# A hybrid attention and retention layer: x kept once until it is modulated, eight heads opened over the first ten k-tiles, and the later adaLN rows as one VectorE stream

## The chip, the cores and the metric

The kernel runs on one core of one Trainium2 chip. The metric is the device time of one execution, in microseconds. The kernel before was timed in three runs: 2550.24 us in the median, 2542.49 to 2552.98. A profiled execution of it stands beside these runs, and all rows below come from that one.

## The reference, cut to what matters

The layer takes 256 latent tokens `x` and 256 context tokens `ctx`, each 4096 wide, in float32:

```
mod = silu(c) @ ada_w + ada_b                       # 4096 -> 3 x 4096: shift, scale, gate
mod_c = silu(c_ctx) @ ada_w[:, :2*D] + ada_b[:2*D]  # shift and scale of the context
h  = rms_norm(x, norm_w)   * (1 + scale) + shift
hc = rms_norm(ctx, norm_w) * (1 + scale_c) + shift_c
proj = h @ w_in                                     # 4096 -> 14336: q, k, v, g of groups A and B
pc   = hc @ (the k and v columns of w_in)
o_d  = differential attention of 8 heads A (latent queries, latent and context keys)
o_r  = retention of 8 heads B (two directions, started from the context's state)
y = concat(o_d * silu(dg), o_r * silu(rg)) @ w_out
return x + gate * y
```

Every element of `h` needs its column's shift and scale, which are sums over all 4096 rows of `ada_w`. The matrices are read once: `ada_w` is 201 MB, `w_in` 235 MB, `w_out` 67 MB.

## The kernel before, in words

**Products.** Inputs are float32 and the products are kept near that precision by splitting each operand into a high and a low part (float32r) and adding three products: hi x hi, hi x lo and lo x hi. `h` is held transposed: 32 k-tiles of 128 rows (columns of the model) by 512 tokens, 256 of them latent and 256 context, in high and low parts (`hh`, `hl`). A tile of `h` is the stationary operand, and the weights stream past it. `prep` (L378) loads two k-tiles of weights into a `raw` buffer (three of them), one DMA for each of the two column segments, makes the high part on ScalarE (L390) and the low part by a subtraction on VectorE (L391), one k-tile at a time. `mm_unit` (L395 on) runs the three products (L404 to L406). A unit is two k-tiles of one head's columns. The k and v columns (kv) need all four row tiles of 128 tokens, the q and gate columns (qg) only the two latent ones; a head of A has 512 columns in each, one of B 384. Queues hold the DMA issues: nearly all loads are issued by SP, in order; stores and small loads by ScalarE's queue.

**Start.** `x` and `ctx` are loaded row by row (`load_x`), squared on ScalarE or VectorE for the norm, transposed on TensorE (L136), and written as a high and a low part into `hh` and `hl` (L363, L364). `rbc` holds each token's 1/rms in every partition.

**First stage, chunks of adaLN.** `K1` is 20: for the first 20 k-tiles shift and scale come from TensorE (`Ada`, L264): `CHUNKS` are 1, 1 and then nine times 2 k-tiles; a chunk has four groups of 16 small matmuls, then eight (`pm`, L280) that bring the sums to the columns' partitions. `modulate` (L283 on) turns a k-tile of x into a k-tile of h: L294 adds high and low part back together, L298 multiplies by norm and scale, ScalarE adds the shift (L299), VectorE forms the low part (L300). In between, the first `NS` = 5 heads of A run their kv units on each chunk as it comes (`SUnit`, L555 to L557); their sums are added up in SBUF by VectorE (L563), and the last head's stays in PSUM.

**Second stage, first parts.** The other 11 heads run kv over k-tiles 0 to 19 (`FIRST`, tiles psA5p to psB7p), and their sums go out to DRAM (`p_dram`). Meanwhile VectorE makes the adaLN sums of the last 12 k-tiles (`ada2_task`: three chunks of four k-tiles, 32 steps each; a step loads 512 KB of `ada_w` and does two accumulations of 128x1024, L325 and L327). At the end of a chunk 32 small matmuls (L335) close it. `between1` sets how many of its steps follow each unit.

**Third stage.** `SCHED`: for each head the kv units of the last 12 k-tiles, added to the stored part (L491, L499), and all 32 k-tiles of qg. The attention of one head (`attA`, `attB`) runs as a task of small steps between the units of the next. The gate (`gate_task`, L918 to L948) goes as VectorE accumulations of 128x512 beside the kv units only. Each head's output is transposed and stored to DRAM (`store_o`).

**Output.** The outputs are loaded back and split (`load_o`, L1015 and L1016), and 128 units run `w_out` with them (tile psO); `out_after` multiplies by the gate and adds x.

**What sets the order.** The program is written in one order; a scheduler works through a model of the time and, on each engine, issues the earliest instruction in program order that is ready, so that work may move ahead of its place where its buffers allow. On the chip each engine then goes strictly in the order found. Pools set the buffers: `a4` (9 places, for head sums, accumulators and outputs), `raw` 3, `whi` and `wlo` 4 single k-tiles, `adaw` 6, PSUM 6 banks for units and 2 for the rest.

Of the kernel before, what the change touches and what calls it, by code (L numbers as in the profile page):

```python
# [38 lines left out]
K1 = 20  # L39
CHUNKS = [1, 1] + [2] * 9  # L40
CHUNKS2 = [4, 4, 4]
LEAD = 0.3
NS = 5
ADAB = 6
RAWB = 3

FIRST = [f"A{h}" for h in range(NS, 8)] + [f"B{h}" for h in range(8)]
SCHED = []
for _h in range(8):
    SCHED += [f"kv A{_h}", f"qg A{_h}"]  # L50
SCHED += ["kv B0", "attB", "qg B0"]
for _h in range(1, 7):
    SCHED += [f"kv B{_h}", f"qg B{_h}"]
SCHED += ["kv B7"]
# [27 lines left out]
def hybrid_kernel(es, tc, x, c, ctx, c_ctx, norm_w, ada_w, ada_b, w_in, q_norm_w, k_norm_w,  # L82
# [12 lines left out]
    a4 = es.enter_context(tc.tile_pool(name="a4", bufs=9, side="right"))  # L95
# [4 lines left out]
    o_dram = dram.tile([HA + HB, P, 2, L], F32, name="o_dram")  # L100
# [3 lines left out]
    for k in "AB":  # L104
        for h in range(8):
            for i in range(2):
                p_dram[f"{k}{h}", i] = dram.tile([P, 2, 512 if k == "A" else 384], F32, name=f"p_dram{k}{h}_{i}")
# [9 lines left out]
    nc.scalar.dma_start(tab, ctab[:, 0:C_J])  # L117
# [21 lines left out]
    hA_cm = tc.tile_pool(name="hA", bufs=1, side="right")  # L139
    hA = hA_cm.__enter__()  # L140
    hB_cm = tc.tile_pool(name="hB", bufs=1, side="right")
    hB = hB_cm.__enter__()
    G = 4
    hh, hl = [], []
    for g in range(KT // G):
        pool = hA if g < KT // G // 2 else hB
        hh.append(pool.tile([P, G, 512], F32R, name=f"hh{g}"))
        hl.append(pool.tile([P, G, 512], F32R, name=f"hl{g}"))

    def h_hi(kt, a, b):  # L150
        return hh[kt // G][:, kt % G, a:b]

    def h_lo(kt, a, b):
        return hl[kt // G][:, kt % G, a:b]

    def load_x(rt):
        src = x if rt < 2 else ctx
        r0 = (rt % 2) * P
        ts = []
        for i in range(4):  # L160
            xt = a4.tile([P, 1024], F32, name=f"x{rt}_{i}", tag="a4")
            nc.sync.dma_start(xt, src[r0:r0 + P, i * 1024:(i + 1) * 1024])
            ts.append(xt)
        return ts

    xts = load_x(0)
# [20 lines left out]
    if True:  # L187
        sp = Carve(wpool.tile([P, 512], F32, name="setup0", tag="wlo", bufs=4))
        cr = sp.tile([64, P], F32, name="cr")
        nc.sync.dma_start(cr[0:32], c[0].rearrange("(k p) -> k p", p=P))  # L190
        nc.sync.dma_start(cr[32:64], c_ctx.rearrange("(k p) -> k p", p=P))
# [23 lines left out]
    c0s2 = [K1 + sum(CHUNKS2[:j]) for j in range(len(CHUNKS2) + 1)]  # L215

# [67 lines left out]
    def modulate(k0, cn, pm):  # L284
# [5 lines left out]
        for k in range(cn):  # L290
            kt = k0 + k
            t = adap.tile([P, 512], F32, name=f"hm{kt}", tag="hm")
            hi, lo = h_hi(kt, 0, 512), h_lo(kt, 0, 512)
            nc.vector.tensor_tensor(t, hi.bitcast(F32), lo.bitcast(F32), op=ALU.add)  # L294
            for s in range(2):
                a, b = s * 256, (s + 1) * 256
                sc, sh = md[:, k, 2 + s:3 + s], md[:, k, s:s + 1]
                nc.vector.scalar_tensor_tensor(t[:, a:b], t[:, a:b], sc, rbc[:, a:b], op0=ALU.mult, op1=ALU.mult)  # L298
                nc.scalar.activation(hi[:, a:b], t[:, a:b], AF.Identity, bias=sh)  # L299
                nc.vector.scalar_tensor_tensor(lo[:, a:b], t[:, a:b], sh, hi[:, a:b].bitcast(F32),  # L300
                                               op0=ALU.add, op1=ALU.subtract)

    def ada2_task():

        work = [(j, k) for j in range(len(CHUNKS2)) for k in range(KT)]
        ahead = []

        def load():
            if len(ahead) < len(work):
                j, k = work[len(ahead)]  # L310
                ahead.append(ada_load(c0s2[j], CHUNKS2[j], k, f"ada2_{j}_{k}")[0])

        for _ in range(ADAB - 1):
            load()
# [783 lines left out]
```

## Time and profile before

| what | value |
|---|---|
| median of three runs | 2550.24 us |
| the profiled execution's own time | 2548.96 us |
| its span, first to last instruction | 2547.1 us |
| mean granted clock of TensorE | 0.993 |
| TensorE busy | 2496.5 us |
| VectorE busy | 1718.8 us |
| ScalarE busy | 1000.9 us |
| moved by DMA | 563.70 MB, 221 GB/s over the span |

A line in the table of groups names line, engine, operation, the tile written and the tiles read, shapes and count; then busy time, mean of one in ns, and the engine's idle time before it. A busy TensorE is not one at its peak, since the ends of matmuls are modelled; how fast it goes is read from the distance of the starts.

### The profile page before, as it was taken

To read this page: it belongs to the slowest core of one execution; us is meant where nothing else is said; L and a number is where in the kernel's file an instruction comes from. 1 tells how busy PE (TensorE), PEld (TensorE's weight loads), DVE (VectorE), ACT (ScalarE), POOL (GpSimd) and SP (SyncE) were. 2 spreads that over 40 slices of the span, in tenths; PEclk is the share of its full clock that TensorE was granted. 3 is DMA by queue.
4 is the path that set the end of the run, shared out by engine and by line. 5 is a ranking of instruction groups with operands and counts; after the bars stand their busy time and mean duration, and the time that the engine had idled before them with its cause. 6 is when DMAs were issued, how large, how long until landed. Compare 5 with 4: busy or idle time off the path is not lost.

```text
span 2547.1 us, 36352 instructions
## 1 busy us (share of the span) xinstructions
PE 2496.5 (98%) x12634; PEld 2125.9 (83%) x12634; DVE 1718.8 (67%) x3028; ACT 1000.9 (39%) x2011; POOL 46.3 (2%) x49
## 2 busy tenths in 40 slices
PE   7899999999999999999999999999999999999999
PEld 4566667888999997788888888899999999788887
DVE  5555556965979546777877887777777666655554
ACT  5222222222323233354445444544444445444443
POOL 0000000000000000000000000000000000000000
PEclk8999999999999999999999999999999999999999
DMA  9989887865777438766776677556666556666765
GB/s 317 300 277 299 279 284 260 292 213 162 246 239 234 143 110 273 235 217 198 240 228 213 203 243 230 178 184 196 199 206 204 165 157 193 195 220 208 225 211 175
DMA packets 495159, 563.70 MB, mean 221 GB/s; under 512 B 31664, under 2 KB 385264, under 8 KB 494976
## 3 DMA queue, kind: packets, MB, share of 16 engines
q1 hardware_dynamic: 478208, 526.54, 65.9%
q10 hardware_dynamic: 16768, 34.85, 4.0%
q8 instruction: 99, 1.62, 0.3%
q14 instruction: 84, 0.69, 0.1%
HBM read 538.17 MB, written 23.09 MB: 220 GB/s over the span
## 4 chain that ended last, share of the span: by engine, by line
PE 90%; DMA 6%; DVE 2%; SPq 1%; issue 1%; ACT 1%; DVEq 0%; POOL 0%; ACTq 0%; POOLq 0%
PE psA L405 8%; PE psA L406 8%; PE psA L404 8%; PE psB L405 6%; PE psB L406 6%; PE psB L404 6%; PE psO L404 5%; PE psO L405 5%; PE psO L406 5%; DMA ada<-in_ada_w_dram 3%; PE pa L264 3%; DMA graw<-in_ada_w_dram 1%; PE psA3s L555 1%; PE psA1s L555 1%; PE psP L556 1%; PE psP L555 1%
## 5 line engine op out<-in xcount | busy, mean ns | idle before, releaser
L390 ACT CAST whiB<-rawB 128x384 fp32r<-128x384 f32 x512 | 259.6, 512 | 471.0 <-PE psB L406 197.9
L390 ACT CAST whiA<-rawA 128x512 fp32r<-128x512 f32 x412 | 253.9, 620 | 425.0 <-PE psA L406 242.0
L391 DVE TENSOR_TENSOR wloB<-rawB,whiB 128x384 fp32r<-128x384 f32 x512 | 279.2, 553 | 173.3 <-ACT whiB L390 169.7
L391 DVE TENSOR_TENSOR wloA<-rawA,whiA 128x512 fp32r<-128x512 f32 x412 | 281.8, 687 | 152.3 <-ACT whiA L390 147.9
L405 PE MATMUL psA<-wloA,hh 128*128 128x512 f32 x896 | 357.6, 399 | 2.1 <-DVE wloA L391 2.1
L406 PE MATMUL psA<-whiA,hl 128*128 128x512 f32 x896 | 355.5, 397 | 0.0
L404 PE MATMUL psA<-whiA,hh 128*128 128x512 f32 x896 | 319.2, 398 | 0.0
L405 PE MATMUL psB<-wloB,hh 128*128 128x384 f32 x896 | 303.7, 339 | 2.2 <-DVE wloB L391 2.2
L406 PE MATMUL psB<-whiB,hl 128*128 128x384 f32 x896 | 302.4, 337 | 0.0
L391 DVE TENSOR_TENSOR wloO<-rawO,whiO 128x512 fp32r<-128x512 f32 x256 | 175.6, 691 | 157.2 <-ACT whiO L390 156.9
L404 PE MATMUL psB<-whiB,hh 128*128 128x384 f32 x896 | 263.9, 339 | 1.2 <-ACT whiB L390 1.2
L390 ACT CAST whiO<-rawO 128x512 fp32r<-128x512 f32 x256 | 158.0, 620 | 200.0 <-PE psO L406 164.0
L327 DVE SCALAR_TENSOR_TENSOR acc<-ada,cT,acc 128x1024 f32<-128x1024 f32 x186 | 233.8, 1277 | 0.0
L937 DVE SCALAR_TENSOR_TENSOR gacc<-graw,cT,gacc 128x512 f32<-128x512 f32 x248 | 184.7, 745 | 51.5 <-DMA graw<-in_ada_w_dram 49.7
L405 PEld LDWEIGHTS psA<-wloA,hh 128*128 128x128 f32 x896 | 168.7, 188 | 42.7 <-DVE wloA L391 4.1
L405 PE MATMUL psO<-wloO,ohh 128*128 128x512 f32 x512 | 203.9, 399 | 0.0
L406 PE MATMUL psO<-whiO,ohl 128*128 128x512 f32 x512 | 203.5, 398 | 0.0
L404 PEld LDWEIGHTS psA<-whiA,hh 128*128 128x128 f32 x896 | 168.5, 189 | 39.7
L406 PEld LDWEIGHTS psA<-whiA,hl 128*128 128x128 f32 x896 | 168.7, 188 | 39.0
L405 PEld LDWEIGHTS psB<-wloB,hh 128*128 128x128 f32 x896 | 169.0, 189 | 4.4 <-DVE wloB L391 3.7
L406 PEld LDWEIGHTS psB<-whiB,hl 128*128 128x128 f32 x896 | 168.9, 189 | 0.3
L404 PE MATMUL psO<-whiO,ohh 128*128 128x512 f32 x512 | 164.0, 399 | 3.9 <-ACT ohh L1015 3.9
(395 smaller groups left out, 4213.3 us busy)
## 6 DMA issues: line engine op xcount, KB each, us to landing
ada<-in_ada_w_dram SPq DMA_DIRECT2D x512, 256.0 KB, 4.8
rawA<-in_w_in_dram SPq DMA_DIRECT2D x412, 256.0 KB, 3.2
rawB<-in_w_in_dram SPq DMA_DIRECT2D x256, 256.0 KB, 3.2
graw<-in_ada_w_dram SPq DMA_DIRECT2D x128, 512.0 KB, 4.9
rawO<-in_w_out_dram SPq DMA_DIRECT2D x128, 512.0 KB, 4.4
rawB<-in_w_in_dram SPq DMA_DIRECT2D x256, 128.0 KB, 2.9
p_dramA<-kvqgA ACTq DMA_DIRECT2D x16, 512.0 KB, 5.1
kvqgA<-p_dramA SPq DMA_DIRECT2D x16, 512.0 KB, 7.6
```

What stands on the lines that cost most here:

```text
L264: m = nc.tensor.matmul(self.pa[32 * g:32 * (g + 1), :], cpad[:, 2 * kt:2 * kt + 32], tiles[k], start=(u0 == 0 and i < 4), stop=(u0 + nk == ...
L327: nc.vector.scalar_tensor_tensor(acc[v], w, cv, acc[v], op0=ALU.mult, op1=ALU.add)
L390: nc.scalar.copy(hi, raw[:, k])
L391: nc.vector.tensor_tensor(lo, raw[:, k], hi.bitcast(F32), op=ALU.subtract)
L404: nc.tensor.matmul(pt[:, :ncol], a, hi, start=f, stop=False)
L405: nc.tensor.matmul(pt[:, :ncol], a, lo, start=False, stop=False)
L406: nc.tensor.matmul(pt[:, :ncol], b, hi, start=False, stop=e)
L555: nc.tensor.matmul(pt, a, hi, start=f, stop=False)
L556: nc.tensor.matmul(pt, a, lo, start=False, stop=False)
L937: nc.vector.scalar_tensor_tensor(acc, raw[:, k], cT[:, 0, kt:kt + 1], acc, op0=ALU.mult, op1=ALU.add)
```

## The change

The diff changes these things together.

- x is loaded by columns (`load_x`, all sixteen loads at once), squared on ScalarE, transposed, and copied once by VectorE into float32 tiles `raws` (two k-tiles each); `modulate` reads these and writes a new tile of `h` (high and low part, one place of `a4`). The tile of x is then free. The tiles of h come free one by one too.
- The pool `a4` has 39 places for all of it.
- `K1` is 10, `CHUNKS` 1, 1 and four times 2; `NS` is 8, so all heads of A open in the first stage.
- `Ada2` makes the adaLN sums of the other 22 k-tiles on VectorE: chunks of 2, 4, 4, 4, 4, 4 k-tiles. `spend` hands it an amount of time after each unit, and it goes as many steps as that pays for, by the costs `T_STEP`.
- `first_parts` goes over the heads (B kv, A qg, B qg, then A kv again) and gives each the k-tiles that are ready by then (`avail`); its sum is stored. `kdone` keeps how far each has come. What is left of the stream after that runs on its own.
- `rests` does the remaining k-tiles of every head, with all stored sums loaded and added (L499 before), the qg sums too.
- `prep` splits both k-tiles of a unit with one conversion and one subtraction; `whi` and `wlo` have three pairs.
- The gate goes in steps of 128x1024, spread evenly over all units of the third stage.
- The outputs of the B heads stay in SBUF as split tiles, and the output projection takes them first, the reloaded ones of A after them.

The diff, cut:

```diff
-K1 = 20
-CHUNKS = [1, 1] + [2] * 9
-CHUNKS2 = [4, 4, 4]
+CHUNKS = [1, 1] + [2] * 4
+K1 = sum(CHUNKS)
+LATER = [2, 4, 4, 4, 4, 4]
+
+FILL = 0.9
+T_COL = 0.457e-3
+T_STEP = {2: 1.49, 4: 2.55}
 LEAD = 0.3
-NS = 5
+NS = 8
...
+SLOTS = 39
...
-    nc.scalar.dma_start(tab, ctab[:, 0:C_J])
+    nc.sync.dma_start(tab, ctab[:, 0:C_J])
...
+    def load_x(src, i):
+
+        xt = a4.tile([P, 2, 512], F32, name=f"x{i}", tag="a4")
+        nc.sync.dma_start(xt, src[:, i * 512:(i + 1) * 512].rearrange("(r p) n -> p r n", p=P))
+        return xt
+
+    NX = D // 512
+    xts = [load_x(x, i) for i in range(NX)] + [load_x(ctx, i) for i in range(NX)]
...
             t = adap.tile([P, 512], F32, name=f"hm{kt}", tag="hm")
-            hi, lo = h_hi(kt, 0, 512), h_lo(kt, 0, 512)
-            nc.vector.tensor_tensor(t, hi.bitcast(F32), lo.bitcast(F32), op=ALU.add)
...
+                nc.vector.scalar_tensor_tensor(t[:, a:b], raw[:, a:b], md[:, k, 2 + s:3 + s], rbc[:, a:b],
+                                               op0=ALU.mult, op1=ALU.mult)
+            hs[kt] = a4.tile([P, 2, 512], F32R, name=f"h{kt}", tag="a4")
...
+        def steps(self):
+            for _ in range(ADAB - 1):
+                self.load()
+            for i, (c0, cn, k0) in enumerate(self.work):
+                n = cn * P
+                if k0 == 0:
+                    acc = [a4.tile([P, 2 * n], F32, name=f"acc{c0}_{v}", tag="a4") for v in range(2)]
+                for k, w in enumerate(self.ahead[i]):
...
+                    yield T_STEP[cn]
+                self.load()
+                if i + 1 == len(self.work) or self.work[i + 1][0] != c0:
...
+                    modulate(c0, cn, pm)
+                    self.avail = c0 + cn
+                    yield cn * 2.0 + 1.0
+
+        def spend(self, us):
+
+            self.credit += us
+            while self.credit > 0 and not self.done:
+                try:
+                    self.credit -= next(self.it)
+                except StopIteration:
+                    self.done = True
...
-        out_ = []
-        for k in range(nk):
-            hi = wpool.tile([P, ncol], F32R, name=f"whi{name}_{k}", tag="whi", bufs=4)
-            lo = wpool.tile([P, ncol], F32R, name=f"wlo{name}_{k}", tag="wlo", bufs=4)
-            nc.scalar.copy(hi, raw[:, k])
-            nc.vector.tensor_tensor(lo, raw[:, k], hi.bitcast(F32), op=ALU.subtract)
-            out_.append((hi, lo))
-        return out_
+        hi = wpool.tile([P, nk, ncol], F32R, name="whi" + name, tag="whi", bufs=3)
+        lo = wpool.tile([P, nk, ncol], F32R, name="wlo" + name, tag="wlo", bufs=3)
+        nc.scalar.copy(hi, raw)
+        nc.vector.tensor_tensor(lo, raw, hi.bitcast(F32), op=ALU.subtract)
+        return [(hi[:, k], lo[:, k]) for k in range(nk)]
...
+        if ada.pos == len(ada_units):
+            ada2.spend(0.3)
...
+    kdone = {(nm, qg): K1 if nm[0] == "A" and not qg else 0 for nm in heads for qg in range(2)}
+
+    def first_parts():
+
+        items = [(f"B{h}", 0) for h in range(HB)] + [(f"A{h}", 1) for h in range(HA)] + [(f"B{h}", 1) for h in range(HB)]
+        for nm, qg in items + [(f"A{h}", 0) for h in range(HA)]:
+            hd = heads[nm]
+            a, b = kdone[nm, qg], ada2.avail
+            if a < b and not (a > 0 and ada2.done):
+                kdone[nm, qg] = b
+                nrt = 2 if qg else 4
+                spare = FILL * 2 * 3 * nrt * hd.ncol * T_COL - (0.2 + 2 * hd.ncol * 1.05e-3)
+                for u in head_units(hd, qg, pairs(a, b), part=True, rest=a > 0, tag=f"p{a}"):
+                    yield u, lambda spare=spare: ada2.spend(spare)
+
+    run_units(first_parts())
+    while not ada2.done:
+        ada2.spend(1.0)
...
+        else:
+            o_t[slot] = a4.tile([P, 2, 2, L], F32R, name=f"o{slot}", tag="a4")
+            split(o_t[slot][:, 0], o_t[slot][:, 1], pt)
...
+    GW = 1024
+    GATE_STEPS = D // GW * (KT + 1)
...
+        gate_due[0] += GATE_STEPS / gate_due[1]
+        while gate_due[0] >= 1:
+            gate_due[0] -= 1
+            next(gate, None)
...
+    def rests():
+        for nm in [f"A{h}" for h in range(HA)] + [f"B{h}" for h in range(HB)]:
+            hd = heads[nm]
+            us = []
+            for qg in range(2):
+                a = kdone[nm, qg]
+                if a < KT:
+                    us.append(head_units(hd, qg, pairs(a, KT), rest=a > 0))
+                else:
+                    load_part(hd, qg)
...
+    order = list(range(HA, HA + HB - 1)) + list(range(HA)) + [HA + HB - 1]
```

## Rows read from the trace of the kernel before

**Rows 1.** The page's first part: span, and busy time of each engine.
```profile
span 2547.1 us, 36352 instructions
PE 2496.5 (98%) x12634; PEld 2125.9 (83%) x12634; DVE 1718.8 (67%) x3028; ACT 1000.9 (39%) x2011; POOL 46.3 (2%) x49
```

**Rows 2.** Table by stage: stretch and length in us, busy, clock, DMA share, GB/s.
```profile
0.00:50.00 50.00, 33.24 (x239) 23.26 (x239) 31.39 (x73) 33.56 (x65) 2.42 (x8) 0.85 1.03 318
50.00:140.00 90.00, 78.83 (x407) 51.02 (x404) 47.01 (x84) 20.24 (x38) 0.00 (x0) 0.95 0.97 308
140.00:434.00 294.00, 286.47 (x1449) 197.01 (x1448) 168.53 (x298) 66.34 (x118) 0.00 (x0) 1.00 0.87 280
434.00:603.00 169.00, 169.00 (x723) 135.87 (x722) 116.72 (x128) 43.90 (x73) 0.00 (x0) 1.00 0.68 220
603.00:941.00 338.00, 338.00 (x1965) 336.44 (x1964) 258.49 (x353) 103.47 (x212) 0.00 (x0) 0.99 0.65 203
```

**Rows 3.** TensorE in order of time, one chunk: start, length, operation, idle before.
```profile
221.47 1.92 PE L264 MATMUL pa<-ada,cpad 128*32 128x512 f32 x16
...
229.52 2.04 PE L264 MATMUL pa<-ada,cpad 128*32 128x512 f32 x16 [1.72 <-DMA ada<-in_ada_w_dram]
...
253.49 0.95 PE L280 MATMUL pm<-tab,ms 128*128 128x2 f32 x8
...
260.56 1.92 PE L264 MATMUL pa<-ada,cpad 128*32 128x512 f32 x16
```

**Rows 4.** TensorE in order of time, first parts: first and last of 67.
```profile
934.82 0.34 PE L405 MATMUL psB7p<-wloB,hh 128*128 128x384 f32 x1
...
946.26 0.34 PE L405 MATMUL psB7p<-wloB,hh 128*128 128x384 f32 x1
```

**Rows 5.** Chain that ended last, 900 to 1000 us: closing matmuls of a chunk.
```profile
906.79 3.46 PE pm L335 x32
```

**Rows 6.** Groups by line, VectorE.
```profile
L391 DVE TENSOR_TENSOR wloA<-rawA,whiA 128x512 fp32r<-128x512 f32 x412 | 281.8, 687 | 152.3 <-ACT whiA L390 147.9 <-DMA rawA<-in_w_in_dram 3.5
L391 DVE TENSOR_TENSOR wloB<-rawB,whiB 128x384 fp32r<-128x384 f32 x512 | 279.2, 553 | 173.3 <-ACT whiB L390 169.7 <-DMA ada<-in_ada_w_dram 1.5
L327 DVE SCALAR_TENSOR_TENSOR acc<-ada,cT,acc 128x1024 f32<-128x1024 f32 x186 | 233.8, 1277 | 0.0
L937 DVE SCALAR_TENSOR_TENSOR gacc<-graw,cT,gacc 128x512 f32<-128x512 f32 x248 | 184.7, 745 | 51.5 <-DMA graw<-in_ada_w_dram 49.7
...
L563 DVE TENSOR_TENSOR kvqgA<-psA1s,kvqgA 128x512 f32<-128x512 f32 x40 | 27.6, 689 | 35.2 <-PE psA1s L557 35.2
```

**Rows 7.** Groups by line, ScalarE.
```profile
L390 ACT CAST whiB<-rawB 128x384 fp32r<-128x384 f32 x512 | 259.6, 512 | 471.0 <-PE psB L406 197.9 <-PE psB3p L406 32.8 <-PE psB0p L406 30.0
L390 ACT CAST whiA<-rawA 128x512 fp32r<-128x512 f32 x412 | 253.9, 620 | 425.0 <-PE psA L406 242.0 <-PE psA6p L406 38.9 <-PE psA5p L406 36.4
```

**Rows 8.** DMA issues, 447 to 545 us (276 GB/s): KB each, us to landing.
```profile
DMA packets 19137, 27.00 MB, mean 276 GB/s; under 512 B 1600, under 2 KB 11072, under 8 KB 19130
...
rawA<-in_w_in_dram SPq DMA_DIRECT2D x36, 256.0 KB, 5.1
```

**Rows 9.** DMA issues, 610 to 850 us (239 GB/s).
```profile
DMA packets 48371, 57.28 MB, mean 239 GB/s; under 512 B 3808, under 2 KB 31968, under 8 KB 48352
...
rawB<-in_w_in_dram SPq DMA_DIRECT2D x55, 256.0 KB, 3.7
```

**Rows 10.** Table by stage for the instructions of tile acc alone.
```profile
500.00:550.00 50.00, 0.00 (x0) 0.00 (x0) 34.89 (x28) 1.00 0.83 267
550.00:600.00 50.00, 0.00 (x0) 0.00 (x0) 0.00 (x0) 1.00 0.36 114
```

**Rows 11.** Waits of TensorE, 434 us to the end: us in total, times, longest.
```profile
PE psO L404 <- ACT ohh L1015: 3.9, 1, 3.9
```

**Rows 12.** TensorE in order of time, a longer wait.
```profile
77.94 2.90 PE L264 MATMUL pa<-ada,cpad 128*32 128x512 f32 x16 [2.48 <-DMA ada<-in_ada_w_dram]
```

**Rows 13.** SP's queue in order of time: the two loads of a B unit.
```profile
1785.27 0.94 SPq L383 DMA_DIRECT2D rawB<-in_w_in_dram  x2
```

More of the change, by code (lines that the diff above doesn't have):

```diff
@@ L375, in hybrid_kernel @@
+        for r in range(2):
+            rt = 2 * half + r
+            dg = adap.tile([P, P], F32, name=f"dg{rt}", tag="hm")
+            nc.vector.tensor_scalar(dg, ident, rs[:, r:r + 1], None, op0=ALU.mult)
+            nc.tensor.matmul(pr[:, rt * P:(rt + 1) * P], ones, dg, start=True, stop=True)
+        ada.load()
+    ada.load()
     nc.scalar.copy(rbc, pr)
@@ L437, in run, with run_units @@
                 self.after()
-    def run_units(units, between=None):
-        for i, u in enumerate(units):
-            u.prepare()
-            if i + 1 < len(units):
-                units[i + 1].prepare()
+    def run_units(units):
+        it = iter(units)
+        nxt = next(it, None)
+        if nxt is not None:
+            nxt[0].prepare()
+        while nxt is not None:
+            (u, post), nxt = nxt, next(it, None)
+            if nxt is not None:
+                nxt[0].prepare()
             u.run()
-            if between is not None:
-                between(i)
+            post()
     class Bank:
@@ L603, in hybrid_kernel @@
     store_part(sheads[-1])
-    ada2 = ada2_task()
-    next(ada2)
-    n_units = len(FIRST) * K1 // 2
-    n_steps = len(CHUNKS2) * (KT + 1)
-    done = [0, 0]
-    def between1(i):
-        done[0] += 1
-        while done[1] < n_steps and done[1] < done[0] / (n_units - 10) * n_steps:
-            next(ada2, None)
-            done[1] += 1
-    for nm in FIRST:
-        run_units(head_units(heads[nm], 0, pairs(0, K1), part=True), between1)
-    for _ in ada2:
-        pass
+    kdone = {(nm, qg): K1 if nm[0] == "A" and not qg else 0 for nm in heads for qg in range(2)}
[13 more added lines that the diff above has]
+        ada2.spend(1.0)
     ada_cm.__exit__(None, None, None)
@@ L925, in gate_task @@
         for v in range(n):
[L926 to L937 removed]
+            cb, kt = divmod(v, KT)
@@ L967, in hybrid_kernel, with between @@
     gate = gate_task()
-    def gate_step():
-        next(gate, None)
-    def between(i):
+    atB = [None]
+    gate_due = [0.0, sum(len(pairs(a, KT)) for a in kdone.values()) - 8]
+    def between():
         bg_step()
@@ L1034, in hybrid_kernel, with load_o, out_ends, start @@
+    run_units(rests())
+    while next(gate, 0) is None:
+        pass
+    def load_o(slot):
+        stg = a4.tile([P, 2, L], F32, name=f"ostg{slot}", tag="a4")
+        nc.sync.dma_start(stg, o_dram[slot])
+        o_t[slot] = a4.tile([P, 2, 2, L], F32R, name=f"o{slot}", tag="a4")
+        split(o_t[slot][:, 0], o_t[slot][:, 1], stg)
     NB = D // 512
     final_units = []
-    def out_after(nb, bank):
-        def f():
+    def out_ends(nb, bank):
+        t = []
+        def start():
             gt = a4.tile([P, 512], F32, name=f"gt{nb}", tag="a4")
```

354 lines of the change are left out of this document (142 added, 212 removed).

## The prediction

> **What bounds it now.** I read the page's first part, then the table by stage, then the order of TensorE's instructions. The first shows TensorE busy for 2496.5 of 2547.1 us [rows 1]; the second shows where the other 51 us lie: 17 before 50 us, 11 from 50 to 140, 7.5 from 140 to 434, none from 434 to 941 [rows 2], so some 15 in all the rest. So two things can pay: less TensorE work, and the waits of the first 434 us. In that stretch DMA is at 0.87 of its engines or more (280 to 318 GB/s); afterwards, up to 941, at 0.65 to 0.68. VectorE is at 69% and 76% from 434 to 941 [rows 2].
>
> The prices. A 512-column matmul takes 0.234 us (720 weight matmuls, 30 units of 24, in 169 us) [rows 2]; a 384-column one 0.1733 (66 starts in 11.44 us) [rows 4]. A unit (two k-tiles) is then 5.62 us for kv and 2.81 for qg of an A head, 4.16 and 2.08 of a B head. A chunk of two k-tiles lasts 39.1 us (221.47 to 260.56): 120 weight matmuls, 28.1; four adaLN groups of 16 at about 1.95, 7.8; eight pm matmuls, 0.8; that leaves 2.4 us, 1.7 of it a wait for an adaLN load [rows 3].
>
> **The change, part by part.**
>
> *adaLN leaves TensorE.* Five of nine two-tile chunks go: 5 x (7.8 + 0.8) = **-43 us**. The VectorE stream gets ten more k-tiles, whose closing matmuls (32 in 3.46 us [rows 5], eight per tile) cost 80 x 0.108 = **+9**. The weight and output matmuls keep their number; when they run is what changes.
>
> *The chunk stage* reads the same 8.4 MB of ada_w per chunk, but beside eight heads instead of five: 12.6 MB in 192 x 0.234 + 8.6 = 53.5 us, 235 GB/s, where 11.0 MB in 39.1 us were 282. The waits of 140 to 434 should go; the earlier ones, where one-tile chunks follow the start, partly stay. Bounds 0 and -18.5 (both idle times of [rows 2]); I take **-10**.
>
> *The start.* Until 50 us DMA is at 1.03 of its engines [rows 2], and the same x, first chunk and weights must arrive before the first weight matmul. That x goes through one VectorE copy and shorter squares takes work off ScalarE and VectorE, which have 33.6 and 31.4 us there; DMA covers it. All x loads now stand before the first adaLN load on SP's queue, which delays the one as much as it advances the other; the loads of c pass to ScalarE's queue and the table to the head of SP's, ahead of x, some 0.1 MB. **0**, bounds -3 and +3. L294's adds leave VectorE, beside TensorE: 0.
>
> *Weight split by pairs.* One conversion and one subtraction replace two each. From the two widths [rows 6, 7] the slopes are 0.84 ns an element on ScalarE and 1.05 on VectorE, so a pair costs 1.05 and 1.22 us (A), 0.83 and 0.96 (B), against 1.37 and 1.11 on VectorE before. Off the path: 0 by itself, but it sets the loop below.
>
> *First parts.* By the kernel's own accounting (spare time per unit: 3.78 us A kv, 2.78 B kv, 1.25 A qg, 0.89 B qg) I followed which k-tiles are ready when each head starts: 44 units B kv, 60 A qg, 72 B qg, 52 second parts of A kv; 794 us of TensorE. What is new is 132 qg units in a row beside the adaLN stream. A raw buffer comes back only after its subtraction, and there are three: issue of two loads (0.94 [rows 13]), landing, conversion, subtraction, and that over three is the fastest unit. Landing is 3.7 us at 239 GB/s [rows 9] and 5.1 at 276 [rows 8]. B qg wants 0.39 MB per 2.08 us (189 GB/s), some 100 of the stream and 20 of stores: more than either row. With 3.7 us its loop is (0.94 + 3.7 + 0.83 + 0.96)/3 = 2.14 us, with 5.1 it is 2.61; over 72 units +4 and +38, and if each subtraction also stands behind one accumulation of 1.28 us [rows 6], 3.04 us and +69. Nothing in the trace has such a run of short units with a stream. The load is nearest to the 276 GB/s row, but the list of the stream is elastic (a late unit leaves it more room), so I take **+20**, bounds 0 and +69. A qg: (0.94 + 5.1 + 1.05 + 1.22)/3 = 2.77 against 2.81: **+2**, bounds 0 and +15. The second parts of A kv take four adds of 0.69 us [rows 6] before their banks come free, with only two spare banks: **+3**, bounds 0 and 8. What is queued behind a late adaLN tile on VectorE is the next weight subtraction, and TensorE waits for that.
>
> *The end of the stream.* Its cost is 64 x 0.745 + 160 x 2.55 + 50 for the modulations = 506 us; the budgets hand out 44 x 2.78 + 60 x 1.25 + 72 x 0.89 + 52 x 3.78 + 3 = 461. Some 43 us of VectorE work stand behind the last first part, with the next head's subtractions behind them. But the stream doesn't keep to its place in the program: before, 33 steps that are meant to last until past 603 were finished at 550 [rows 10]. VectorE's whole work there is 112 x 1.22 + 116 x 0.96 = 248 of subtractions, 22 of adds and 506 of stream, 776 against 794 + 20 on TensorE, and in the last chunks it has idle time too. So I take **+3** for the last modulation, bounds 0 and +42.
>
> *The rest.* Sixteen qg sums are stored, loaded and added; A kv once more. 32 additions on VectorE, which has fewer subtractions to do; loads on SP and stores on ScalarE's queue come four units early: 0. The gate is spread over the qg units also: a B qg unit with 0.54 steps of 0.52 MB is at some 290 GB/s, as above, but six or eight such units stand between kv units twice as long, and three split pairs are ahead: 0, bound +14. The a4 pool has 39 places: after the first parts 10 k-tiles of h are dead, so 22 + two heads (6) + gate (4) fit, and at the end 20 + 6 + 4 + seven finished outputs: 0. In the output projection the wait of 3.9 us for the reloaded last head [rows 11] goes, since B's outputs stay on the chip: **-4**, bounds -4 and +2. POOL's powers are two instead of four, and nothing new waits for them: 0.
>
> **Sum.** -43 + 9 - 10 + 20 + 2 + 3 + 3 - 4 = -20. The profiled execution took 2548.96 us, 1.9 more than its span; so 2529 by it, and 1.3 more by the median of the runs (2550.24): **2530 us**.
>
> **The rivals.**
> A. *All hidden*: the loop keeps up, because a raw tile that is asked for early lands as in the 239 GB/s row. -43 + 9 - 18 - 4 = -56 at best, with small losses -35: 2494 to 2515. For it: no idle from 434 to 941 with VectorE at 76% [rows 2]. Against: those units are twice as long. 0.2.
> B. *The stream ends late*: VectorE can't run ahead, because adaLN buffers or DMA hold it. Then up to 42 stand bare, while the B qg loop, with less beside it, costs 10: -20 - 10 + 39 = +9, 2559; half of it, 2540. 0.13.
> C. *Slower*: the loop of B qg decides alone. From 2.08 + 0.75 = 2.83 us per unit on (each subtraction behind an accumulation at 5.1 us landing gives 3.04) it costs 54 to 69 instead of 20: 2564 to 2579. The place is the stretch with 72 B qg units. 0.14.
> D. *The clock*: waits in that stretch could be long enough to slow TensorE. After a wait of 2.48 us the next adaLN group took 2.90 us [rows 12], after one of 1.72 us 2.04 [rows 3], so short waits cost nothing here, long ones do; a loop 0.3 to 0.9 us late per unit stays under both. If all 72 units ran at half the clock, 72 x 2.08 = 150 more: 2680. 0.03. The Trainium skill (TensorE: Matmul & The Clock Gate, HAM oscillation) tells of a matmul with little work per load whose every load wait put the engine back to half its clock, so that each step began cold; that speaks against thin units beside a stream. By it the sum would be D's, by the rows it is mine.
> E. *The first stage gains nothing*: DMA still limits it, because the first one-tile chunks need as many bytes and their waits grow. -10 falls away and some 5 are added: 2545. 0.05.
>
> **From cases to numbers.** The forecast's own range is 2515 to 2545, 0.45. About 0.5% (12.8 us) is what a measurement of this kernel can tell from no change: faster ends at 2537.5, slower begins at 2563. Faster: 0.2 (A) + 0.34 of the forecast + 0.01 of B = 0.55. Same: 0.11 of the forecast + 0.11 of B + 0.05 (E) = 0.27. Slower: C, D and 0.01 of B = 0.18. The range leaves out about a tenth on either side: 2495 to 2572.
>
> **What would show it.** Right: adaLN groups on TensorE 24 instead of 44; the chunk stage over at about 325 us with under 2 us idle per chunk; acc instructions well ahead of their heads; B qg first units at some 2.35 us each with raw loads landing in 4 to 5 us; no wait over 10 us at the last pm. Wrong: B qg at 2.8 us or more (C); TensorE idle for tens of us while VectorE accumulates, after the last A kv part (B); granted clock under 0.95 between 600 and 850 us (D); idle over 15 us before 320 us (E); first parts without idle (A).

## The result, and the profile after

The changed kernel takes 2660.06 us (median of 4 runs, 2654.71 to 2661.88) where the kernel before took 2550.88 (4 runs on the same chip, 2542.49 to 2552.98): 1.043 times as long, 95% interval 1.040 to 1.046. I had forecast 2530 and a range up to 2572. The profiled run took 2661.34 us, 112 more than that of before, at a span of 2659.6.

The page of the changed kernel, its first part, beside [rows 1]:

```profile
span 2659.6 us, 33974 instructions
PE 2515.6 (95%) x12354; PEld 2140.1 (80%) x12354; DVE 1820.5 (68%) x2438; ACT 887.6 (33%) x1384; POOL 42.7 (2%) x47
```

TensorE has 280 matmul records fewer, and is still busy 19 us longer: part of that time was spent at the lower clock (mean granted clock 0.969, before 0.993). It is idle for 144 us where it was idle for 51. The table by stage of the changed kernel (columns as in [rows 2]) says where:

```profile
0.00:50.00 50.00, 33.55 (x225) 21.74 (x226) 27.38 (x62) 26.13 (x74) 1.61 (x6) 0.83 1.05 320
50.00:140.00 90.00, 86.90 (x449) 58.02 (x448) 55.99 (x91) 24.95 (x41) 0.00 (x0) 0.98 0.94 295
140.00:250.00 110.00, 110.00 (x543) 76.74 (x542) 63.39 (x92) 22.11 (x27) 0.00 (x0) 1.00 0.78 249
250.00:350.00 100.00, 98.35 (x452) 81.94 (x451) 91.13 (x136) 23.01 (x30) 0.00 (x0) 1.00 0.78 263
350.00:1160.00 810.00, 794.84 (x3877) 693.74 (x3877) 630.16 (x639) 255.36 (x321) 2.90 (x1) 1.00 0.78 256
...
1186.00:1220.00 34.00, 24.98 (x91) 19.70 (x91) 28.53 (x50) 7.72 (x12) 0.00 (x0) 0.75 0.33 103
1220.00:1282.00 62.00, 41.88 (x140) 30.14 (x139) 47.36 (x63) 15.04 (x35) 2.50 (x1) 0.78 1.03 366
1842.00:1945.00 103.00, 47.88 (x191) 36.33 (x192) 60.28 (x133) 31.26 (x81) 5.82 (x7) 0.65 0.22 81
```

The first five rows are what the prediction was about, and they went much as forecast. The last three are three stalls, all in or at the third stage, for which the forecast had 3 us. What a stretch loses I read as its length less busy time times granted clock (an estimate, since the ends of matmuls are modelled): 34 - 24.98 x 0.75 = 15 us, 62 - 41.88 x 0.78 = 29 and 103 - 47.88 x 0.65 = 72. Together 116 us.

**Stall 1, 1186 to 1220: the stream's end.** TensorE in order of time (start, length, operation, idle before):

```profile
1197.06 0.79 PE L406 MATMUL psA<-wloA,h 128*128 128x512 f32 x1 [4.08 <-DVE wloA L393]
...
1204.49 6.56 PE L330 MATMUL pm<-ones,acc 128*128 128x1 f32 x30 [0.84 <-DVE acc L322]
```

The third stage has begun, its units wait for weight subtractions that stand behind the last accumulations on VectorE, and the last closing matmuls run at the lower clock (0.50 from 1204 to 1212): 30 take 6.56 us where 32 took 3.46 [rows 5].

**Stall 2, 1220 to 1282: a burst on the queue.** DMA issues of the changed kernel from 1233 to 1282 us (KB each, median us to landing):

```profile
DMA packets 8001, 19.09 MB, mean 390 GB/s; under 512 B 696, under 2 KB 4223, under 8 KB 7997
...
graw<-in_ada_w_dram SPq DMA_DIRECT2D x21, 512.0 KB, 9.1
rawA<-in_w_in_dram SPq DMA_DIRECT2D x16, 256.0 KB, 8.3
kvqgA<-p_dramA SPq DMA_DIRECT2D x8, 512.0 KB, 9.2
```

The gate's loads, meant as one every other unit, come 21 in 49 us, and with them 8 stored sums for several heads at once. A weight load takes 8.3 us to land where it took 5.1 at 276 GB/s [rows 8]. TensorE waits up to 6.4 us for a conversion (the first of the waits below; 14.2 of its 17.6 us lie here).

**Stall 3, 1842 to 1945: A7's attention, alone.** The attentions run one after another, as a chain in which each is a link; one stands bare when no unit's matmuls run beside it. Each attention of an A head has one long power on POOL near its start, so POOL's instructions in order of time are a list of them (start, length; the last row is near the end of A7's):

```profile
1265.12 2.50 POOL L749 TENSOR_TENSOR rsA<-rsA,mhalf 128x12 f32<-128x12 f32 x1 [120.38 <-DMA graw<-in_ada_w_dram]
...
1648.23 2.58 POOL L749 TENSOR_TENSOR rsA<-rsA,mhalf 128x12 f32<-128x12 f32 x1 [9.76 <-DVE rsA L748]
...
1859.78 2.58 POOL L749 TENSOR_TENSOR rsA<-rsA,mhalf 128x12 f32<-128x12 f32 x1 [7.14 <-DVE rsA L748]
...
1896.77 0.54 POOL L826 TENSOR_TENSOR stA<-stA,mhalf 128x1 f32<-128x1 f32 x1 [2.17 <-DVE stA L825]
```

The same rows of the kernel before, first and last of eight:

```profile
1039.66 2.56 POOL L736 TENSOR_TENSOR rsA<-rsA,mhalf 128x12 f32<-128x12 f32 x1 [92.73 <-DVE rsA L735]
...
1657.12 2.58 POOL L736 TENSOR_TENSOR rsA<-rsA,mhalf 128x12 f32<-128x12 f32 x1 [9.79 <-DVE rsA L735]
```

And TensorE's instructions on the third stage's sums, changed kernel (times, first and last start):

```profile
L405 PE MATMUL psA<-whiA,h x560: 387/397/796, 1163.5 to 1646.2; 128*128 128x512 f32 x187
...
L405 PE MATMUL psB<-whiB,h x896: 332/336/689, 1646.9 to 2278.9; 128*128 128x384 f32 x180
```

Before, A's sums ran from 956 to 1648 us (692), and the eight attentions started one every 88 us: when the sums ended, the last attention was just starting (1657). After, A's sums last 484 us, but the attentions still start one every 85 us ((1859.78 - 1265.12) / 7); beside A's sums it is even 96 ((1648.23 - 1265.12) / 4), and 71 after them. When A's sums end at 1647, the fifth of the eight attentions is just starting. TensorE runs ahead with B's sums for 195 us and then stops, until A7's attention is over and B's have begun, which the program puts behind it. The waits of the changed kernel (us in total, times, longest; the first three of TensorE in the whole span, the last of SP's queue from 1842 to 1960):

```profile
PE psA L405 <- ACT whiA L392: 17.6, 7, 6.4
PE kTpA L132 <- DVE kvqgA L718: 12.2, 1, 12.2
PE psA L406 <- DVE wloA L393: 11.9, 8, 4.1
...
SPq L387 <- DVE nlbB L862: 59.0, 1, 59.0
```

The second is TensorE at the start of A7's attention. The last is SP's queue from 1842 on: the next weight load stands for 59 us, as VectorE makes no weight subtraction between 1843 and 1901, only A7's steps. From 1842 to 1930 TensorE runs no unit.

### The profile page after: what moved, and what is told of

The parts are those of the page before. It is cut to its first block, busy times and chain, and to the rows that moved or that the text cites. A ratio compares the mean times of both kernels' runs of the same rounds, so it can differ in the third digit from the quotient of the medians.

```text
span 2659.6 us, 33974 instructions
## 1 busy us (share of the span) xinstructions
PE 2515.6 (95%) x12354; PEld 2140.1 (80%) x12354; DVE 1820.5 (68%) x2438; ACT 887.6 (33%) x1384; POOL 42.7 (2%) x47
## 5 line engine op out<-in xcount | busy, mean ns | idle before, releaser
L322 DVE SCALAR_TENSOR_TENSOR acc<-ada,cT,acc 128x1024 f32<-128x1024 f32 (+1 forms) x372 | 427.9, 1190 | 0.0
L406 PE MATMUL psB<-wloB,h 128*128 128x384 f32 x896 | 305.2, 341 | 2.4 <-DVE wloB L393 2.4
L407 PE MATMUL psB<-whiB,h 128*128 128x384 f32 x896 | 303.3, 339 | 0.0
L405 PE MATMUL psB<-whiB,h 128*128 128x384 f32 x896 | 285.1, 340 | 5.7 <-DVE kvqgB L500 5.7
L406 PE MATMUL psA<-wloA,h 128*128 128x512 f32 x560 | 229.4, 410 | 12.0 <-DVE wloA L393 11.9
L405 PE MATMUL psA<-whiA,h 128*128 128x512 f32 x560 | 212.8, 405 | 17.6 <-ACT whiA L392 17.6
L407 PE MATMUL psA<-whiA,h 128*128 128x512 f32 x560 | 226.0, 406 | 0.0
L406 PE MATMUL psO<-wloO,o 128*128 128x512 f32 x512 | 204.1, 399 | 0.3 <-DVE wloO L393 0.3
L407 PE MATMUL psO<-whiO,o 128*128 128x512 f32 x512 | 203.4, 398 | 0.0
L405 PE MATMUL psO<-whiO,o 128*128 128x512 f32 x512 | 184.3, 399 | 1.2 <-ACT o L722 1.2
L952 DVE SCALAR_TENSOR_TENSOR gacc<-graw,cT,gacc 128x1024 f32<-128x1024 f32 x124 | 158.8, 1281 | 38.7 <-DMA graw<-in_ada_w_dram 37.6
L405 PEld LDWEIGHTS psB<-whiB,h 128*128 128x128 f32 x896 | 167.7, 190 | 7.5 <-DVE kvqgB L500 6.1
L406 PEld LDWEIGHTS psB<-wloB,h 128*128 128x128 f32 x896 | 169.3, 189 | 4.9 <-DVE wloB L393 4.0
L407 PEld LDWEIGHTS psB<-whiB,h 128*128 128x128 f32 x896 | 169.4, 189 | 0.5
```

The costliest lines, as they stand in the source:

```text
L322: nc.vector.scalar_tensor_tensor(acc[v], w, cv, acc[v], op0=ALU.mult, op1=ALU.add)
L405: nc.tensor.matmul(pt[:, :ncol], a, hi, start=f, stop=False)
L406: nc.tensor.matmul(pt[:, :ncol], a, lo, start=False, stop=False)
L407: nc.tensor.matmul(pt[:, :ncol], b, hi, start=False, stop=e)
L952: nc.vector.scalar_tensor_tensor(acc, raw, cT[:, 0, kt:kt + 1], acc, op0=ALU.mult, op1=ALU.add)
```

## The experiments

Sixteen kernels; each time stands beside runs of the kernel before on the same chip (2550 to 2553). "Changed" is 2660, and "less" and "more" are against it where nothing else is named. Kernels 5 and 6 leave out part of the layer's work, and so return another result.

**1. The pace of the attention steps.**

```diff
-        bg_step()
-        if len(tasks) > 1:
+        for _ in range(3):
             bg_step()
```

> Three attention steps are issued behind every unit instead of one or two. Theory P (the pace of issue sets the length of the chain of attentions): A's eight attentions, some 79 us each in the changed kernel (1265 to 1900), shrink to about 60, the length of a head's sums, A7's attention no longer runs alone after 1842, and the time falls by 55 to 75 us, to about 2595. Theory C (the chain is long because its dependent instructions stand in line behind other work on VectorE, ScalarE and TensorE, and A's sums of the third stage, 484 us instead of 690, are too few to cover it): 70 to 76 us each, A7 still alone for about 40 us, and the time falls by 10 us at most: 2650 to 2660.

2705.24 us: 45 more, outside both. The first and the last power of A's attentions on POOL, and the table by stage of this run:

```profile
1265.72 2.50 POOL L749 TENSOR_TENSOR rsA<-rsA,mhalf 128x12 f32<-128x12 f32 x1 [118.89 <-DMA kvqgA<-p_dramA]
...
1829.96 2.58 POOL L749 TENSOR_TENSOR rsA<-rsA,mhalf 128x12 f32<-128x12 f32 x1 [7.13 <-DVE rsA L748]
```

```profile
1800.00:1920.00 120.00, 59.98 (x238) 45.95 (x239) 69.15 (x150) 35.05 (x90) 5.82 (x7) 0.64 0.21 76
1960.00:2400.00 440.00, 407.34 (x2205) 383.99 (x2204) 268.92 (x397) 141.79 (x213) 6.50 (x12) 0.93 0.58 188
```

A7 is still alone, and earlier. The attentions start 81 us apart instead of 85, so theory P is out: issuing them sooner hardly shortens them. What neither theory had is the second row: B's part loses 440 - 407.34 x 0.93 = 61 us. In the changed kernel the same stretch loses 22 (426.88 us busy at 0.98). It goes in dents of 5 to 10 us, most at a change of B heads; in this stretch TensorE waits 9.6 us for conversions, 5.9 for subtractions and 9.1 for the rope of B's attentions on VectorE (L881). I read it as the run ahead with B's sums being shorter here (145 us instead of 195); that wasn't tested alone.

**2. The gate late.**

```diff
-        gate_due[0] += GATE_STEPS / gate_due[1]
+        if atB[0] is not None:
+            gate_due[0] += GATE_STEPS / gate_due[1]
```

(and the divisor counts B's units alone)

> The gate's steps are issued only after the change to B's attentions, one per unit, none beside A's units. Theory G (the gate's burst of 32 loads and accumulations makes the stall of 1233 to 1282): that stretch loses its 20 us of idle time and its half clock, and the time falls by 25 to 40 us, to about 2630. It also takes 1.28 us accumulations out of VectorE's line, so the attentions of A should take about 72 us each instead of 79. Rival (the stall comes from the switch to 24-matmul units with their stored sums to add, not from the gate): no change there, 2650 to 2665. In B's part VectorE takes 164 us more beside some 620 us of sums, where it was at 60 to 68 per cent: no cost expected there by either.

2719.24 us: 59 more, a miss. Table by stage:

```profile
1186.00:1282.00 96.00, 79.00 (x305) 61.15 (x304) 56.98 (x97) 25.46 (x50) 2.50 (x1) 0.88 0.62 210
1780.00:1900.00 120.00, 50.04 (x172) 33.43 (x171) 65.93 (x150) 36.46 (x92) 5.82 (x7) 0.57 0.19 63
1940.00:2080.00 140.00, 119.72 (x630) 114.54 (x629) 102.20 (x140) 38.48 (x60) 2.16 (x4) 0.88 0.69 241
```

Where the gate left, theory G holds in part: 1186 to 1282 loses 26 us instead of 45. Where it went it costs more, 35 us in 1940 to 2080 alone, in a part where I had expected none, from VectorE's average. And the stall at A7 is no smaller (91 us lost in these 120, 75 in the 120 from 1842 on of the changed kernel): it doesn't need the gate. A7's power comes 43 us earlier here (1816), but TensorE runs ahead with B's sums for only 149 us (1627 to 1776). What ends that run ahead I didn't test.

**3. The change to B's attentions at B2 instead of B0** (`if nm == "B2":`, with B0's and B1's attentions kept back until then).

> The change from A's to B's attentions is issued at the fifth unit of B2 instead of B0; B0's and B1's attentions wait until then. Theory D (the early drain puts all of A7's steps in TensorE's order without a unit between them): A7's attention runs beside B units, the idle 55 to 60 us of 1842 to 1945 fall to 15 to 25 (B0's and B1's attentions now come close together), and the time falls by 30 to 50 us, to about 2620. Theory C (the chain is too long for the sums beside it, and the places of the a4 pool end the run ahead wherever the drain stands): the wait moves to B0's and B1's attentions and the time falls by 0 to 20 us, 2640 to 2660.

2638.17 us: 22 less, just above theory C's 20 and short of theory D's 30. Table by stage:

```profile
1900.00:2020.00 120.00, 80.55 (x391) 70.82 (x390) 80.64 (x164) 39.62 (x78) 4.40 (x8) 0.74 0.31 103
```

A loss of 60 where 72 were lost; the rest of the gain is in smaller dents. TensorE runs ahead with B's sums until 1915 instead of 1841, so A7 is covered, and the wait has moved to B0's and B1's attentions, as theory C said.

**4. More of each unit for the stream** (`FILL = 1.0`).

> The share of a unit's time that the stream may use goes from 0.9 to 1.0; the budgets then hand out about 538 us where the stream needs 506. Theory S (the stream's end stands bare at 1186 to 1210): the last chunk ends among the first parts, the 10 to 15 us of idle time there and the half clock go, and the time falls by 10 to 25 us, to about 2642. Rival (VectorE can't go faster, and more of the stream per unit only moves the waits into the first parts): idle between 750 and 900 grows by what the end loses, 2655 to 2670.

2633.27 us: 27 less. Table by stage:

```profile
1180.00:1280.00 100.00, 93.81 (x384) 74.20 (x383) 73.57 (x117) 29.27 (x50) 5.39 (x2) 0.95 0.85 300
...
1840.00:1960.00 120.00, 65.05 (x295) 52.25 (x294) 73.03 (x152) 36.67 (x88) 5.82 (x7) 0.69 0.27 94
```

Stall 1 and most of stall 2 go together: 11 us lost in place of 45. The first parts give back some of it (87.82 of 100 us busy from 720 to 820, where the changed kernel has 93.23), and the stall at A7 stays as it was (the second row). The 10 to 25 expected was short because stall 2 hung on the stream's end too, which I hadn't seen.

**5. The rope of A's heads left out** (the two calls of `rope_maps`).

> The rope of A's heads is left out (two times 4 x 0.286 + 2 x 0.69 = 2.5 us on VectorE per head, 5 us), all else as in the changed kernel. Theory C (A's attentions are one chain, longer than the sums beside it): each link gets 5 to 10 us shorter, the last one starts 35 to 70 us earlier while B's sums still have places, and the part of it that stands alone shrinks: 30 to 60 us less, 2600 to 2630. Rival (it is the place of the drain, which sets A7's attention alone whatever its length): 5 to 10 us less, 2650 to 2655.

2625.5 us: 35 less, inside theory C and far beyond the rival's 10. Table by stage:

```profile
1840.00:1920.00 80.00, 50.56 (x252) 44.03 (x251) 55.27 (x102) 24.44 (x45) 2.16 (x4) 0.77 0.43 141
```

With shorter links (78 us on average) the bare part shrinks: it loses 41 us instead of 72.

**6. An eighth of the gate** (`GK = 4` k-tiles in place of 32).

> Of the gate's 32 k-tiles per column block only 4 are summed, so 112 of 128 loads of 0.52 MB and accumulations of 1.28 us are left out (143 us of VectorE, 59 MB). Theory G' (the gate's bursts of loads, at 1.0 of the DMA engines and 360 to 400 GB/s, hold up the weights beside them wherever they stand): the idle of 1233 to 1282 falls from 20 to under 8 us, the dents of 1480 to 1500 and 2020 to 2060 go, and A's attentions take some 73 us each, as with the late gate; the stall of A7 stays, since it stood there with the late gate as well. In all 40 to 60 us less: 2600 to 2620. Rival (the first units of the third stage stall by their stored sums and the setup, not by the gate): 0 to 15 us less.

2610.96 us: 49 less, so seven eighths of the gate's loads and accumulations cost that much here. (The kernel before carries the gate too, so this is more than what spreading it cost.) But stall 2 keeps a core. Table by stage, and DMA issues from 1235 to 1262 us of this run:

```profile
1240.00:1260.00 20.00, 6.54 (x23) 4.21 (x22) 3.73 (x3) 1.72 (x2) 0.00 (x0) 0.67 1.04 398
```

```profile
kvqgA<-p_dramA SPq DMA_DIRECT2D x10, 512.0 KB, 10.2
rawA<-in_w_in_dram SPq DMA_DIRECT2D x8, 256.0 KB, 8.1
```

With little of the gate left (three of its loads here), ten stored sums of 0.5 MB, for the kv and qg of several heads at once, stand beside the weights' loads, which land as late, and TensorE is busy for 6.54 of 20 us. The change has both: more sums stored, and the gate beside them. A7's stall stays, though smaller: 1820 to 1900 loses 49 us (45.54 busy at 0.67).

**7. No A head opens its qg sums early**, share 1.0 (the item `(f"A{h}", 1)` leaves the list of first parts).

> A's qg sums aren't opened early (60 units go back to the third stage), with the share at 1.0 as in the run before: A's sums of the third stage are then 618 us, as good as the 629 of the kernel before by the same count. Theory C: A7's attention runs beside B's sums, and from 1500 us to the output projection TensorE is idle for under 15 us. The stream then has 560 us of first sums beside it where its 506 us and some 150 of subtractions want 650, so 80 to 110 us of idle come up in the first parts and at the end of the stream. In all 2633 - 70 + 95 = 2655, from 2635 to 2680. Rival (the stall has another cause): the same idle at the stream and the stall of 55 to 60 us at A7 as well, 2710 to 2740.

2596.26 us: 64 less, and 37 less than run 4, from which it differs by this one edit; better than expected, and the decisive run. POOL in order of time, and the table by stage:

```profile
1711.20 2.58 POOL L749 TENSOR_TENSOR rsA<-rsA,mhalf 128x12 f32<-128x12 f32 x1 [10.78 <-DVE rsA L748]
...
1772.96 0.54 POOL L826 TENSOR_TENSOR stA<-stA,mhalf 128x1 f32<-128x1 f32 x1 [3.08 <-DVE stA L825]
```

```profile
940.00:1060.00 120.00, 88.63 (x288) 64.35 (x288) 113.37 (x136) 21.84 (x30) 0.00 (x0) 0.72 0.64 199
...
1690.00:1830.00 140.00, 140.00 (x836) 138.98 (x836) 87.62 (x163) 55.09 (x108) 6.79 (x7) 1.00 0.47 143
```

A7's attention lies between 1690 and 1830, where TensorE isn't idle at all: stall 3 is gone by giving A's sums back (run 4, with the same share, has it in full). In its place the stream's end is bare: from 940 to 1060 VectorE is busy 113 of 120 us and TensorE loses 56.

**8. Experiments 3 and 4 together.**

> The two runs that gained, together: the change to B's attentions at B2, and the share at 1.0. If their stalls are separate, the gains add up: 2660 - 22 - 27 = 2611. If the share's gain only moves sums that the chain of attentions then lacks: 2620 to 2635.

2624.39 us. The gains don't add: 1900 to 2020 loses 66 us (75.31 busy at 0.72), more than in 3. I read that as share 1.0 also moving sums out of the third stage (B's first products there number 848 in the trace instead of 896).

**9. Only A0 to A3 open qg early**, share 1.0.

> Only A0 to A3 open their qg sums early, share 1.0. Theory C with its numbers from the run where no A head did: the chain of A's attentions needs about 100 us to its first link and 8 x 77 us; A's sums of the third stage (461 us by the same count as 629 in the kernel before) and the 130 us of B's sums that went ahead in every run just about cover it, so no attention stands alone for over 15 us. The stream has some 85 us more of first sums beside it than with none opened, which takes most of the 60 us lost from 940 to 1040 there. 2596 - 50 = 2546, from 2535 to 2575. Rival (the two stalls are one shortage of sums for VectorE's and the chain's work together, and each sum moved takes from one what it gives to the other): 2585 to 2600.

2617.62 us, a miss: 72 above the forecast, and 18 above the rival's range. The stream's end is covered (230 of 230 us busy from 900 to 1130), and A7 is covered, but the four short heads now come first: A3's attention stands bare among A's own sums (one wait of 16.4 us for L718, as at A7 before; 1360 to 1460 busy 66.91 at 0.80), and 1560 to 1660 loses 32 us more (81.06 busy at 0.84). The mechanism is the same, only its place moved: what counts is the sums beside each attention, not their total.

**10. Only A4 to A7 open qg early**, share 1.1.

> Only A4 to A7 open their qg sums early, share 1.1: by the count of the compiled order 55 us fewer first sums beside the stream than with A0 to A3 and share 1.0, and 545 instead of 461 us of A's sums left. Theory C: nothing bare at A7; the stream's end costs 20 to 40 us more than with A0 to A3: 2565 to 2585. Rival (the last heads' sums are the ones that cover the chain, so opening those brings the stall back): 2600 or more.

2577.38 us, as expected: nothing bare at A7, 1186 to 1282 busy 95.60 of 96 us; what is left is idle in the first parts (106.18 of 120 from 640 to 760) and at the change to B (1840 to 1920: 59.82 of 80 at 0.85).

**11. Four raw buffers**, with 38 places (`RAWB = 4`).

> The changed kernel with four raw buffers and 38 places. Theory L (the term of +20 in the prediction: three raw buffers set the fastest B qg unit beside the stream): the idle of some 13 us from 740 to 860 falls under 4 and the time by 8 to 12 us, 2648 to 2652. Rival (there DMA is at 0.97 of its engines and 307 to 317 GB/s, and a further load only waits longer to land): the idle stays above 9 us, landing of a raw load gets about a quarter longer, and the time stays within 5 us or rises by the place that is gone.

2617.15 us: 43 less, four times what I expected. Table by stage of this run, then of the changed kernel:

```profile
740.00:860.00 120.00, 117.94 (x649) 113.34 (x648) 115.06 (x119) 52.98 (x72) 0.00 (x0) 1.00 0.96 314
1186.00:1282.00 96.00, 86.25 (x338) 68.03 (x337) 77.14 (x113) 27.21 (x54) 2.50 (x1) 0.87 0.87 312
```

```profile
740.00:860.00 120.00, 108.67 (x592) 101.59 (x590) 111.77 (x116) 46.91 (x66) 0.00 (x0) 1.00 0.91 289
1186.00:1282.00 96.00, 66.86 (x230) 49.84 (x230) 75.89 (x112) 22.77 (x47) 2.50 (x1) 0.77 0.78 273
```

Theory L holds: the idle of the B qg stretch falls from 11.3 to 2.1 us, at more GB/s, not less. And the same loop of three buffers had a part in stalls 1 and 2: 21 us lost there instead of 45. The stall at A7 stays (1800 to 1920: 65.58 busy at 0.69, 75 lost).

**12 and 13. Four raw buffers on 10 and on 7.**

> A4 to A7 alone open qg early, share 1.1, and four raw buffers with 38 places. Loop theory: the fourth buffer takes away the idle of the first parts (some 14 us from 640 to 760) and 5 to 10 us of the third stage's first units, as it did in the changed kernel, and nothing of what it gained there at A7 (which isn't bare here): 2577 - 22 = 2555, from 2545 to 2562, the same as before. Rival (the 43 us came from the stall at A7, whose start the fourth buffer moved): 2570 to 2580.

> No A head opens qg early, share 1.0, four raw buffers. Loop theory: from 2596 the 10 us of idle of 520 to 620 go; at the end of the stream (940 to 1040, 50 us lost with VectorE busy all the time) VectorE is the bound and a raw buffer can't help: 2596 - 15 = 2581, from 2570 to 2588. Rival (there too the weights come late, not VectorE): 2540 to 2565.

2564.99 and 2599.83 us. In both the idle of the first parts shrinks as the loop theory says (12, 640 to 760: 115.91 of 120 busy instead of 106.18; 13, 520 to 640: 115.23 instead of 107.19). But 12 gains 12 us of the 22, for A1's attention now stands bare from 1260 to 1320 (47.10 of 60 busy at 0.86, where 10 had 58.09 at 1.00). And 13 gains none: its stream's end (940 to 1060: 87.73 of 120 at 0.72) is VectorE's, busy for 107 of these 120, and at the third stage's sums new dents of 5 us took what was won. Its 2581 was wrong; where those dents come from I didn't follow.

**14. As 12, with the change to B at B1.**

> As the first of this call, with the change to B's attentions at the fifth unit of B1 instead of B0. Theory D (what is left lost from 1840 to 1920, some 18 us, comes from the place of the drain): 8 to 15 us less than the first. Rival (it is the first B attention waiting for A7's end, wherever it is issued): within 5 us of the first.

2557.2 us (12 runs), 1.0019 times the kernel before (1.0008 to 1.0030): 8 less than 12, at the foot of theory D's range and outside the rival's 5. But 1840 to 1920 loses 20 us (67.60 busy at 0.89) where 12 lost 24 (63.80 at 0.87), so only some 5 us came from there, and of the 18 that theory D put down to the place of that change most stay.

**15 and 16. As 14, with share 1.2; and with A3 to A7 opening qg early.**

> As the last run (A4 to A7 open qg early, four raw buffers, change to B at B1), share 1.2. In the compiled order no attention of A stands without units, but 60 us fewer first sums lie beside the stream. Theory (both covers count, and sums moved from one are missed by the other): the 19 us of 1260 to 1320 go, the end of the stream costs 15 to 35 us: 2553 to 2573. Rival (VectorE keeps up with 60 us less beside it): 2535 to 2545.

> As the last run, with A3 to A7 opening qg early, share 1.1: 897 instead of 904 us of first sums, and in the compiled order one short bare stretch at the change to B (31 instructions on TensorE) in place of that of 1260 to 1320 (29). Theory: the one loss takes the place of the other, 2550 to 2560. Rival (at the change to B it is hidden behind B0's and B1's sums): 2538 to 2548, faster than before.

2567.18 us, as theory said, and 2562.0, 2 us above its range. In 15 the bare attention of 1260 to 1320 is gone (59.82 of 60 busy), and the stream shows instead: 7.97 of 20 us busy from 900 to 920, with VectorE at 19.32. In 16 it is gone too (59.68 of 60), but the loss at the change to B stays as in 14 (1860 to 1920: 46.52 of 60 at 0.86), and a new one of 11 us shows at the stream's end (1040 to 1060: 14.03 of 20 at 0.65). None of the sixteen beats the kernel before.

## Why the prediction was wrong

The bill, by the profiled runs: forecast -20, measured +112. The three stalls are 116 where the forecast had 3, the first parts 15 where it had 25, the chunk stage -14 where it had -10. Smaller dents of the third stage and the output (2020 to 2060, 1480 to 1500, 2320 to 2340) come to some 16 more than before, and the -4 of the output falls away. That makes 99; another 13 I can't place. Part of them may lie in the -34 of adaLN, a count times a price that I didn't read off the changed kernel.

**Right.** *adaLN off TensorE*: 24 groups (384 matmul records) instead of 44. *The chunk stage*: it is over at 325 us, where B0's first unit starts, and idle from 50 to 350 us is 4.8 us; before it was 18.7 to 434 [rows 2]. *The start*: 16.5 us idle, as before. *The loop of three raw buffers*: +20, and +2 for A qg, stood against 15.2 us of idle in all first parts, with B's larger raw loads landing in 3.4 to 4.6 us (740 to 860); experiment 11 shows that it was this loop. Rival C didn't come. Rival D didn't come where I put it: the clock there is 1.00. In stall 2 it did: raw loads landed in 8.3 us, and after the wait of 6.4 us the granted clock was 0.50 (1245 to 1250). The Trainium skill's picture of it (TensorE: Matmul & The Clock Gate, HAM oscillation), waits for loads that make each next step start cold, agrees with that.

**Mis-sized: "The end of the stream", +3 with bounds 0 and +42.** It cost 15 (stall 1) and helped to make stall 2. This was rival B, with stall 1 at about a third of its 42. I argued from an average: 776 us of VectorE work against 814 of TensorE. Experiment 4 shows the price of the place in the program, which I had written off: with more of the stream done earlier, 45 us lost became 11.

**Wrong: "The rest", the step that summed the third stage.** Two of its sentences failed, and a third is open.
- *"32 additions on VectorE ...; loads on SP and stores on ScalarE's queue come four units early: 0."* I counted what the stored sums add and not what their absence takes away. A's third stage went from 692 to 484 us, and its sums were the cover of eight attentions that follow each other every 85 us. I never costed that chain, because before it had just fitted and so showed no wait: 72 us, stall 3. Experiments 5 and 7 show it from both sides, a shorter chain and more cover.
- *"The gate is spread over the qg units also: ... 0, bound +14."* Spread in the program, it came in bursts, 21 loads in 49 us. The bound was taken for an even pace. With the stored sums and the stream's end it is stall 2, 29 us; without the gate (experiment 2) stalls 1 and 2 lose 26 together instead of 45.
- *"The a4 pool has 39 places ...: 0."* Places, as I counted them, were enough for heads in step. They were not asked what happens with three heads of B waiting for A7. Whether they end the run ahead there, no run tested.

*The output, -4*: the wait for the reloaded last head is gone, but B7's attention now ends bare (oTpB, two waits of 4.4 us in all, against the 3.9 of [rows 11]), so nothing was gained.

The marks of "what would show it" were on the first two stages and the stream's end. I had none for the attentions of the third stage, since I had given them no term.

What the best repaired version comes to I read the same way. Where the cover is balanced (14), the time is 2557, some 27 above the forecast, and the sums seem not to suffice: the 776 us of VectorE work want as many of sums beside them, A's attentions want some 630 to 700 at their own place (eight links of 79 us in experiment 2, of 88 before), and the 34 us that adaLN was to save on TensorE (-43 + 9) go into the gaps between. Runs 7, 9, 10, 15 and 16 each moved sums from one to the other and found the loss again on the other side. That this is the limit of the idea, and not of the versions I tried, isn't shown. The Trainium skill (Perfetto Trace Analysis, Optimization Strategy) says that interleaving stretches with different most-contended engines may improve performance. The change does so for the stream; experiments 5 and 7 add that the matmuls used for it were already interleaved with something else.

## What to carry to other kernels

When work is moved ahead to cover one thing, ask what it covered where it stood, and give that chain a price even if it shows no wait: number of links times their spacing, against the work that is left beside them. An even rate in the program is not an even rate on a queue; cost a background load by the burst that its buffers allow, at the shortest units it can meet. Averages over a stage (VectorE 776 us against 814, DMA at some 290 GB/s) said "free" of stretches that stalled here.

## What I had not expected of the hardware

A bare chain costs more than TensorE's idle time. From 1842 to 1945 it was idle for 55 us and lost 72, for the mean granted clock there was 0.65, nearer the lower of its two levels (1.2 of 2.4 GHz). It fell after 1849, when TensorE was busy for little over 1 us in 18, and from 1867 to 1917, with the chain's short matmuls between waits, it stayed at 0.50 to 0.64. And DMA moved 390 GB/s over 49 us where the kernel before never needed more than some 318 over a stage [rows 2]; at that rate, with the DMA engines' busy share at 1.03 (1220 to 1282), a load of 0.26 MB took 8.3 us to land.
